# Attention with cosine scores on one core: the written-out instruction orders of the later pairs are replaced

## The chip, the core and the metric

The kernel runs on one core of a Trainium2 chip. The core has five engines with a queue each: TensorE (PE, with its weight loads shown as PEld), VectorE (DVE), ScalarE (ACT), GpSimd (POOL) and SyncE (SP), which issues the transfers. The metric is the device time of one execution in microseconds (us), and the median of several runs is compared.

## The reference

Queries and keys are divided by their norms, the scores are multiplied by 1/tau = 10, and a softmax over the keys weighs the values. There are 8 x 12 heads of 512 positions and 64 dimensions.

```python
Q_norm = Q / (np.linalg.norm(Q, axis=-1, keepdims=True) + 1e-10)
K_norm = K / (np.linalg.norm(K, axis=-1, keepdims=True) + 1e-10)
scores = np.einsum('bhqd,bhkd->bhqk', Q_norm, K_norm) / tau
weights = np.exp(scores - np.max(scores, axis=-1, keepdims=True))
weights = weights / (np.sum(weights, axis=-1, keepdims=True) + 1e-10)
return np.einsum('bhqk,bhkd->bhqd', weights, V).astype(np.float32)
```

## The kernel before

Two heads make a pair, and there are 48 pairs, s = 0 to 47. The work of a pair is a fixed set of operations. The names below are those of the program, and the line is the one that the profile shows.

- LD(s,0), LD(s,1), LV(s): the queries, keys and values are loaded, issued by SyncE (L311, L314). ST(s) stores the result (L569).
- SQ(s,0): GpSimd squares queries and keys at once (L337). RED(s,w): VectorE sums the squares, for w = 0 (queries) and 1 (keys); most sums of the keys are first folded on TensorE by SSQ(s,1) (L354), and then VectorE reduces less (L361 in place of L365).
- NEW(g,k): VectorE finds the reciprocal roots for a group of pairs in steps (L389 to L398).
- SCL(s,w): the scaling to unit length, of queries on VectorE, of keys mostly on GpSimd (both L420).
- TR(s,w): TensorE transposes (L426). EVA(s): VectorE copies the transposes out of the one bank that holds them (L434).
- SCO(s,c): the scores of chunk c (128 keys) for both heads, two matmuls on TensorE (L508).
- EXP(s,c): ScalarE's exponential of those 1024 columns (L531).
- VC(s): GpSimd converts the values (L536).
- PV(s,h,i): four matmuls of the weighted sum (L550); eight such operations make a pair. RCP(s,h) and NRM(s,h): VectorE divides by the sum (L563, L565).

In the pairs 37 and 45 the exponential of chunk 3 isn't ScalarE's. TensorE makes these scores one head at a time in a bank of its own (SCX(s,0), SCX(s,1), L468), VectorE splits each (X(s,h,0), X(s,h,1), L473 and L475), and the polynomial follows: Y(s,0) to Y(s,3) on GpSimd (L479, L480), Y(s,4) and Y(s,5) on VectorE (L486, L480). X(s,0,1) has to be over before SCX(s,1), which writes the same bank.

The scores have two places, so SCO of one chunk waits for the end of the EXP two chunks earlier. PV(s+1,h,0) waits for NRM(s,h), which frees its bank.

Nothing is decided at run time. The dictionary `ORDER` holds one string for each engine, the numbers of the operations in the order in which that engine's queue gets them; a negative number stands for a filler matmul at the start. `Program.schedule` turns the strings into lists, and `write` puts a wait on a semaphore before an operation where another engine has to be done first. Each queue runs strictly in the order written: an operation that waits holds up all behind it on its engine.

```python
for e, text in ORDER.items():
    order[e] = [self.list[int(x)] if x[0] != "-" else self.dummy(int(x[1:])) for x in text.split()]
```

Of the kernel before, what the change touches and what calls it, by code (L numbers as in the profile page):

```python
# [643 lines left out]
def slack(s, most):  # L644
# [14 lines left out]
    ),  # L659
    "pool": (  # L660
# [7 lines left out]
    ),  # L668
    "dve": (
# [24 lines left out]
    ),  # L694
# [33 lines left out]
    ),  # L728
    "act": (
# [44 lines left out]
```

## Time and profile before

| | us |
|---|---|
| median of 3 runs | 189.68 (189.59 to 189.91) |
| the profiled execution | 189.45 |
| its span in the trace | 187.7 |
| ScalarE busy | 180.8 (96%) |
| TensorE busy | 173.8 (93%) |
| VectorE busy | 173.2 (92%) |
| GpSimd busy | 166.8 (89%) |

The span is that of the instructions; what lies around it makes up the rest of the profiled execution's time. Busy times of one engine are a union, so instructions that overlap in their pipeline count once. A row of the timeline gives the start, the time from start to end, the engine, the line, the operation, the tiles and shapes and the count; rows of one line that follow each other are put together.

### The profile page before, as it was taken

The page shows a single profiled execution, that of the slowest core. Times are in us where ns is not written, and L with a number is a line of the kernel's source. Part 1 is how long each engine was busy: PE and PEld are TensorE (multiplying, and loading weights), DVE is VectorE, ACT ScalarE, POOL GpSimd, SP SyncE. Part 2 cuts the span into 40 slices and gives each one's busy share as a digit, 9 for nine tenths or more (in the row PEclk, how much of TensorE's full clock was granted, in tenths as well). Part 3 has the DMA queues.
Part 4 walks back from the last instruction along what each step waited for, and adds up shares of the span by engine and source line. Part 5 has one row for each costly group of instructions (what it writes and reads, how often), then busy time and mean ns, then how long its engine had stood idle before and what let it go on. Part 6 is the DMA issues. An engine that isn't in the chain of part 4 may idle for free.

```text
span 187.7 us, 6646 instructions
## 1 busy us (share of the span) xinstructions
PE 173.8 (93%) x2694; PEld 108.9 (58%) x2694; DVE 173.2 (92%) x546; ACT 180.8 (96%) x212; POOL 166.8 (89%) x152
## 2 busy tenths in 40 slices
PE   6898999999999999999999999999999889998983
PEld 2455666566665666666666556556655446665642
DVE  2788999999999999999999999999999999999864
ACT  4899999999999999999999999999999999999992
POOL 4699999999999999999999999999999999774700
PEclk9999999999999999999999999999999999999999
DMA  5999999899999978999999998899989323112324
GB/s 169 349 351 351 348 357 318 267 326 357 380 386 373 322 248 276 337 334 333 375 380 381 357 334 269 277 291 267 293 279 292 122 88 115 55 61 66 110 65 159
DMA packets 52446, 50.76 MB, mean 270 GB/s; under 512 B 3136, under 2 KB 52416, under 8 KB 52416
## 3 DMA queue, kind: packets, MB, share of 16 engines
q1 hardware_dynamic: 51984, 50.02, 81.2%
q8 instruction: 21, 0.34, 0.8%
q10 hardware_dynamic: 432, 0.33, 0.5%
q14 instruction: 9, 0.07, 0.1%
HBM read 37.75 MB, written 12.58 MB: 268 GB/s over the span
## 4 chain that ended last, share of the span: by engine, by line
ACT 73%; PE 12%; DVE 9%; DMA 3%; issue 1%; SPq 1%
ACT et L531 72%; PE ops L550 4%; PE scps L508 4%; DMA qk<-in_Q_dram 3%; PE tps L426 2%; DVE qn L420 2%; DVE ob L565 2%; DVE xz L475 1%; DVE qt L434 1%; DVE et L486 1%; PE tps L468 1%; DVE xp L473 1%; DVE nps L365 1%; PE ops L580 1%; SPq L311 0%
## 5 line engine op out<-in xcount | busy, mean ns | idle before, releaser
L531 ACT ACTIVATE et<-scps 128x1024 bf16<-128x1024 f32 (+1 forms) x191 | 174.6, 1136 | 0.2
L337 POOL TENSOR_TENSOR sq<-qk 128x1024 bf16<-128x1024 f32 x44 | 82.7, 1892 | 0.6 <-DMA qk<-in_K_dram 0.4
L508 PE MATMUL scps<-qt 64*128 64x512 bf16 x380 | 74.9, 386 | 7.2 <-ACT et L531 3.9
L550 PE MATMUL ops<-vb,et 128*128 128x65 bf16 x1504 | 74.0, 195 | 0.7 <-ACT et L531 0.4
L550 PEld LDWEIGHTS ops<-vb,et 128*128 128x128 bf16 x1504 | 56.0, 98 | 28.6 <-issue 20.9
L420 POOL TENSOR_TENSOR qn<-qk,rk 128x512 bf16<-128x512 f32 x36 | 38.0, 1068 | 2.1 <-DVE rk L394 1.7
L565 DVE TENSOR_TENSOR ob<-ops,rd 128x256 f32<-128x256 f32 x94 | 38.9, 418 | 0.4
L420 DVE TENSOR_TENSOR qn<-qk,nps 128x512 bf16<-128x512 f32 x58 | 38.6, 678 | 0.5 <-ACT nps L382 0.5
L434 DVE COPY qt<-tps 128x1024 bf16<-128x1024 bf16 x47 | 32.2, 686 | 1.9 <-PE tps L426 1.5
L426 PE MATMUL tps<-ident,qn 128*128 128x128 bf16 x376 | 33.7, 221 | 0.2
L508 PEld LDWEIGHTS scps<-qt 64*128 64x128 bf16 x380 | 19.0, 92 | 24.7 <-ACT et L531 10.1
L365 DVE TENSOR_REDUCE nps<-sq 128x8 f32<-128x512 bf16 x48 | 32.3, 683 | 0.0
L536 POOL TENSOR_SCALAR vb<-vf 128x512 bf16<-128x512 f32 x48 | 29.8, 634 | 0.2
L426 PEld LDWEIGHTS tps<-ident,qn 128*128 128x128 bf16 x376 | 21.4, 98 | 12.9 <-issue 6.4
L563 DVE RECIPROCAL rd<-ops 128x4 f32<-128x4 f32 x94 | 16.3, 175 | 3.3 <-PE ops L550 2.5
L354 PE MATMUL ops<-sq,ident 128*128 128x64 bf16 x368 | 18.4, 194 | 0.0
L354 PEld LDWEIGHTS ops<-sq,ident 128*128 128x128 bf16 x368 | 13.8, 98 | 3.4 <-issue 2.3
L361 DVE TENSOR_REDUCE nps<-ops 128x8 f32<-128x64 f32 x40 | 8.5, 213 | 0.1
L480 POOL TENSOR_TENSOR xz<-xz 128x1024 f32<-128x1024 f32 x2 | 3.8, 1892 | 3.4 <-DVE xz L475 3.4
L389 DVE TENSOR_TENSOR nps<-nps,ys 128x32 f32<-128x32 f32 (+1 forms) x30 | 6.3, 209 | 0.1
L390 DVE SCALAR_TENSOR_TENSOR nps<-nps,ys 128x32 f32<-128x32 f32 (+1 forms) x30 | 6.2, 208 | 0.1
L331 POOL TENSOR_TENSOR sq<-qk 128x512 bf16<-128x512 f32 (+1 forms) x4 | 3.7, 932 | 1.0 <-DMA qk<-in_K_dram 0.9
(61 smaller groups left out, 63.7 us busy)
## 6 DMA issues: line engine op xcount, KB each, us to landing
vf<-in_V_dram SPq DMA_DIRECT2D x48, 256.0 KB, 5.3
qk<-in_Q_dram SPq DMA_DIRECT2D x47, 256.0 KB, 4.7
qk<-in_K_dram SPq DMA_DIRECT2D x47, 256.0 KB, 5.6
out_dram<-ob SPq DMA_DIRECT2D x47, 256.0 KB, 4.0
qk<-in_Q_dram SPq DMA_DIRECT2D x2, 128.0 KB, 2.7
qk<-in_K_dram ACTq DMA_DIRECT2D x2, 128.0 KB, 2.9
out_dram<-ob SPq DMA_DIRECT2D x1, 128.0 KB, 1.7
out_dram<-ob ACTq DMA_DIRECT2D x1, 64.0 KB, 1.6
```

What stands on the lines that cost most here:

```text
L337: lambda e: e.tensor_tensor(out=sqf, in0=data, in1=data, op=ALU.mult))
L354: last = e.matmul(out=o_ps[bank][:, 320:384], lhsT=ident[:, :], rhs=sq[iqs][:, 8 * w : 8 * w + 8, 8 * k : 8 * k + 8], start=(k == 0), stop ...
L365: lambda e, w=w, dst=dst: e.tensor_reduce(out=dst, in_=sq[iqs][:, 8 * w : 8 * w + 8, :], axis=AX.X, op=ALU.add))
L420: lambda e, w=w, r=r: e.tensor_tensor(out=qn[iqn][:, w].rearrange("p t h d -> p h t d"), in0=qk[iq][:, w].rearrange("p h (t d) -> p h t d" ...
L426: last = e.transpose(t_ps[:, w, t, :], qn[iqn][:, w, t].rearrange("p h d -> p (h d)"), ident[:, :])
L434: lambda e: e.tensor_copy(out=qt[iqt][:, :, :, :].rearrange("p w t x -> p (w t x)"), in_=t_ps[:, :, :, :].rearrange("p w t x -> p (w t x)")))
L508: last = e.matmul(out=sc_ps[:, 2 * b + h, :], lhsT=qt[iqt][64 * h : 64 * h + 64, 1, c, :], rhs=qt[iqt][64 * h : 64 * h + 64, 0, :, :], sta ...
L531: lambda e, c=c, b=b, hs=hs: e.activation(out=et[iet][:, c, hs[0] : hs[-1] + 1, :], in_=sc_ps[:, 2 * b + hs[0] : 2 * b + hs[-1] + 1, :], f ...
L536: lambda e: e.tensor_scalar(out=vb[:, iq, :, :, 0:DIM].rearrange("p c h d -> p h c d"), in0=vf[iv][:, :, :].rearrange("p h (c d) -> p h c ...
L550: last = e.matmul(out=o_ps[h][:, 65 * t : 65 * t + 65], lhsT=et[iet][:, c, h, 128 * t : 128 * t + 128], rhs=vb[:, iq, c, h, :], start=(i = ...
L563: lambda e, h=h, grid=grid: e.reciprocal(out=rd[io][:, h, :], in_=grid[:, :, DIM]))
L565: lambda e, h=h, grid=grid: e.tensor_tensor(out=ob[io][:, h], in0=grid[:, :, 0:DIM], in1=rd[io][:, h, :].unsqueeze(2).to_broadcast([128, N ...
```

## The change

Only the strings of three engines in `ORDER` differ. ScalarE's and SyncE's stay as they are. The set of operations, their waits, tiles and buffers stay too: the same numbers stand in another order. 389 of TensorE's 735 places, 252 of VectorE's 546 and 71 of GpSimd's 148 hold another operation than before. The first place that differs is TR(15,0), just before the scores of pair 14, on TensorE, RED(19,0) on VectorE and SCL(17,1) on GpSimd.

The core of the diff, GpSimd's string and the last part of TensorE's:

```diff
     "pool": (
...
-        "437 350 395 471 361 318 488 530 426 460 564 607 641 502 536 683 513 717 579 547 759 590 793 836 655 689 "
-        "870 624 666 904 742 731 765 700 938 981 808 819 776 876 1015 1049 910 1083 853 887 921 1125 1066 953 "
-        "1159 987 964 1021 1193 1227 1270 998 1304 1032 1097 1131 1338 1165 1108 1371 1142 1199 1321 1253 1176 "
-        "1414 1459 1242 1210 1493 1397 1526 1310 1343 1287 1603 1421 1386 1637 1569 1465 1354 1670 1712 1436 1757 "
-        "1437 1442 1438 1439 1476 1575 1552 1791 1620 1509 1809 1774 1609 1586 1653 1695 1642 1684 1719 1763 1796 "
+        "437 350 395 471 361 318 488 530 426 460 564 607 641 502 536 683 513 717 579 547 759 590 793 836 655 624 "
+        "870 689 666 904 731 776 700 765 938 887 921 742 808 981 1015 819 998 876 1049 1083 910 853 1125 953 1021 "
+        "987 1032 1159 964 1193 1227 1270 1304 1108 1338 1097 1287 1131 1066 1371 1199 1165 1414 1142 1493 1176 "
+        "1242 1310 1459 1354 1526 1210 1253 1321 1397 1343 1603 1386 1637 1421 1569 1670 1465 1712 1436 1437 1757 "
+        "1438 1442 1439 1476 1575 1791 1509 1695 1552 1609 1740 1586 1653 1620 1642 1809 1684 1719 1774 1763 1796 "
...
     "pe": (
...
-        "1204 1177 1178 1183 1179 1180 1206 1184 1185 1186 1275 1208 1416 1245 1277 1247 1211 1212 1213 1214 1461 "
-        "1249 1311 1217 1309 1251 1218 1219 1220 1279 1344 1342 1281 1254 1260 1255 1256 1283 1261 1262 1257 1263 "
+        "1112 1117 1140 1118 1200 1168 1198 1170 1143 1149 1150 1172 1144 1145 1146 1373 1174 1151 1152 1241 1202 "
+        "1243 1204 1183 1177 1178 1184 1206 1185 1179 1180 1416 1208 1186 1245 1277 1275 1247 1211 1212 1213 1214 "
...
```

Read back into names, TensorE's queue around the scores of pair 35 and of pairs 43 to 47:

```
before: SCO(35,0) PV(33,1,3) SCX(37,0) PV(34,0,0) SCO(35,1) PV(34,0,1) PV(34,0,2) PV(34,0,3) SSQ(41,1)
        SCO(35,2) SCX(37,1) PV(34,1,0) SCO(35,3) PV(34,1,1) PV(34,1,2) PV(34,1,3) SCO(36,0)
after:  SCO(35,0) SCX(37,0) PV(33,1,2) PV(33,1,3) SCO(35,1) PV(34,0,0) PV(34,0,1) SCO(35,2) PV(34,0,2)
        SCX(37,1) SCO(35,3) PV(34,0,3) SSQ(41,1) PV(34,1,0) SCO(36,0)
before: SCO(43,3) PV(42,0,2) SCX(45,1) PV(42,0,3) SCO(44,0) SCO(44,1) ... SCO(45,0) PV(43,1,0) PV(43,1,1)
        TR(47,1) PV(43,1,2) PV(44,0,0) PV(43,1,3) SCO(45,1) TR(47,0) SCO(45,2) PV(44,0,1) PV(44,1,0)
        PV(44,0,2) PV(44,0,3) PV(44,1,1) PV(44,1,2) PV(44,1,3) SCO(46,0) SCO(46,1)
after:  SCO(43,3) PV(42,0,1) PV(42,0,2) SCO(44,0) SCX(45,1) PV(42,0,3) SCO(44,1) ... SCO(45,0) PV(43,1,2)
        PV(43,0,3) PV(43,1,3) SCO(45,1) TR(47,0) TR(47,1) SCO(45,2) PV(44,0,0) PV(44,0,1) PV(44,0,2)
        SCO(46,0) PV(44,0,3) PV(44,1,0) PV(44,1,1) PV(44,1,2) PV(44,1,3) SCO(46,1)
```

GpSimd's queue around the polynomial of pair 37, and VectorE's from X(37,1,1) to the copy of pair 40:

```
GpSimd before: SQ(45,0) Y(37,0) SQ(46,0) Y(37,1) VC(37) Y(37,2) Y(37,3) VC(38) SCL(41,1) VC(40) SQ(47,0)
GpSimd after:  SQ(45,0) Y(37,0) Y(37,1) SQ(46,0) Y(37,2) VC(37) Y(37,3) VC(38) SCL(41,1) SQ(47,0) VC(39)
VectorE before: RCP(34,1) NRM(34,0) X(37,1,1) NRM(34,1) RED(43,0) SCL(39,0) RED(42,1) RCP(35,0) NEW(17,0)
        NRM(35,0) RCP(35,1) NEW(17,1) RED(44,0) NEW(17,2) NRM(35,1) NEW(17,3) SCL(39,1) NEW(17,4) EVA(38)
        NEW(17,5) RED(46,0) RCP(36,1) NEW(17,6) NEW(17,7) NRM(36,1) SCL(41,0) RCP(36,0) NEW(17,8) NRM(36,0)
        EVA(39) SCL(40,1) Y(37,4) SCL(40,0) Y(37,5) EVA(40)
VectorE after:  NRM(34,0) X(37,1,1) RCP(34,1) RED(44,0) RED(43,0) SCL(39,0) RED(42,1) NRM(34,1) RCP(35,0)
        NEW(17,0) NRM(35,0) NEW(17,1) EVA(38) NEW(17,2) SCL(39,1) RCP(35,1) RCP(36,0) NEW(17,3) NRM(35,1)
        NEW(17,4) RED(46,0) EVA(39) NEW(17,5) NRM(36,0) NEW(17,6) NEW(17,7) RCP(36,1) NEW(17,8) SCL(41,0)
        NRM(36,1) SCL(40,1) Y(37,4) SCL(40,0) Y(37,5) EVA(40)
```

Of GpSimd's conversions of values, VC(19), VC(22), VC(23), VC(25), VC(33) and VC(35) stand 7 to 18 places earlier, and VC(27), VC(32) and VC(34) 9 to 16 places later.

82 rows, old and new, of the table ORDER are left out of this document.

## The prediction

> **What bounds the kernel now.** I read the page's groups first. ScalarE's exponentials fill the span, and the idle time put down to them is 0.2 us.
>
> ```profile
> L531 ACT ACTIVATE et<-scps 128x1024 bf16<-128x1024 f32 (+1 forms) x191 | 174.6, 1136 | 0.2
> ...
> L434 DVE COPY qt<-tps 128x1024 bf16<-128x1024 bf16 x47 | 32.2, 686 | 1.9 <-PE tps L426 1.5
> ...
> L563 DVE RECIPROCAL rd<-ops 128x4 f32<-128x4 f32 x94 | 16.3, 175 | 3.3 <-PE ops L550 2.5
> ...
> vf<-in_V_dram SPq DMA_DIRECT2D x48, 256.0 KB, 5.3
> ```
>
> That 0.2 misleads, because the exponentials overlap in their pipeline: one can start late without the engine counting as idle. So I read the chain of work that ended last, in order of time, then the windows restricted to this line, and one exponential alone in the timeline.
>
> ```profile
> 14.79 119.22 ACT et L531 x130
> 134.00 0.04 issue
> ...
> 137.84 0.69 DVE xp L473
> ...
> 154.42 0.42 DVE ob L565
> ...
> 170.22 0.02 issue
> 170.24 11.24 ACT et L531 x12
> ```
>
> ```profile
> 134.00:170.24 36.24, 36.08 (x39) 1.00 0.47 151
> ```
>
> ```profile
> 170.24 1.02 ACT L531 ACTIVATE et<-scps 128x1024 bf16<-128x1024 f32 x1
> ```
>
> Up to 134.00 the rhythm is 119.22 / 130 = 0.917 us for each exponential. From the end at 134.00 to the end of the one that starts at 170.24 (171.26) there are 39 + 1 = 40, which at 0.917 need 36.68; they took 37.26, so 0.58 is lost. The last row's 12 need 1.02 + 11 x 0.917 = 11.11 and took 11.24: 0.13 lost. So about **0.71 us**, 0.37% of the time, is what any order can win on ScalarE, besides a few hundredths hidden in the mean of 0.917. Between the two ScalarE rows the chain runs through TensorE, then through VectorE (from 137.84 to 154.84), then through TensorE again. There the others feed ScalarE too late, though hardly any of them has room:
>
> ```profile
> 135.00:150.00 15.00, 13.89 (x202) 8.17 (x200) 14.78 (x45) 14.99 (x17) 14.88 (x11) 1.00 0.75 239
> ```
>
> The columns are busy times of PE, PEld, DVE, ACT and POOL: VectorE 14.78 of 15, GpSimd 14.88.
>
> The tail cannot change much: the last product's matmuls start 0.05 behind the last exponential's end (183.12 + 1.23 = 184.35), not behind other TensorE work.
>
> ```profile
> 183.12 1.23 ACT L522 ACTIVATE et<-scps 128x256 bf16<-128x256 f32 x3
> ...
> 184.40 0.24 PE L580 MATMUL tps<-vb,et 128*128 128x65 bf16 x2
> ```
>
> **TensorE's part of the change.** A score can start when the exponential two back has ended, and it must start early enough. Prices come from the timeline, start to next start:
>
> ```profile
> 138.34 0.54 PE L550 MATMUL ops<-vb,et 128*128 128x65 bf16 x12
> 138.71 0.40 PE L354 MATMUL ops<-sq,ident 128*128 128x64 bf16 x8
> 139.04 0.39 PE L508 MATMUL scps<-qt 64*128 64x512 bf16 x2
> ```
>
> ```profile
> 169.81 0.39 PE L508 MATMUL scps<-qt 64*128 64x512 bf16 x2
> ```
>
> ```profile
> 174.74 0.40 PE L426 MATMUL tps<-ident,qn 128*128 128x128 bf16 x4
> 175.07 0.39 PE L508 MATMUL scps<-qt 64*128 64x512 bf16 x2
> 175.39 1.03 PE L550 MATMUL ops<-vb,et 128*128 128x65 bf16 x28
> 176.35 0.39 PE L508 MATMUL scps<-qt 64*128 64x512 bf16 x2
> ```
>
> Three PV take 138.71 - 138.34 = 0.37, so 0.123 each. A score takes 175.39 - 175.07 = 0.32. Seven PV ahead of a score take 0.96, which is 7 x 0.123 + 0.10: changing over to a score costs 0.10. A fold (SSQ) or a transpose (TR) ahead of a score takes 0.33, so 0.23 without the change-over. A score of the polynomial's chunk is counted like a score, 0.32.
>
> The limit: the score at 169.81 lets its exponential start at 170.24, 0.43 later, and alone that lasts 1.02. The end is due 2 x 0.917 = 1.83 after the place came free, so a score may start 1.83 - 1.45 = **0.38** after that without loss. Each slot of 0.917 has 0.917 - 0.32 = 0.60 for other work; what is over carries into the next slot.
>
> With the two strings read back into names I added up the slots. From pair 23 on, 23 of 98 slots before hold 0.69 or more, the fullest 0.96 (ahead of SCO(46,0), the row at 175.39) and 0.94 (ahead of SCO(45,1)). After, 11 do, and the fullest has 0.82. Carried from slot to slot, the delay of the score reaches the limit of 0.38 before at SCO(45,1) and SCO(46,0), and 0.37 at four others; over 0.30 it is in 10 slots. After, it never exceeds 0.28 (at SCO(40,2), whose slot is unchanged). The other side is pairs 14 to 22: five slots grow to 0.69 or more from at most 0.59, and the delay rises to 0.28, which still leaves 0.10. The work and its change-overs add up to the same in both. Scores that stand later, behind work that used to wait behind them, cost nothing while the delay stays under 0.38; if 0.1 of other waits falls into the slots at 0.28, each 0.1 more is 0.1 lost.
>
> By TensorE's own time alone the order before loses about 0.1; the rest of the 0.71 comes where a wait on VectorE falls into a slot that is nearly full. In pair 35 SCX(37,0) and SCX(37,1) are involved, in pair 40 NRM(37,1) (the chain's 154.42), at 170.24 SCX(45,1), which stood ahead of SCO(44,0) while X(45,0,1) was running. After, SCX(45,1) stands behind SCO(44,0), and while it waits only PV(42,0,3) and SCO(44,1) queue behind it, whose turn comes later anyway. I count all these as gone but for 0.08 at SCO(40,2) and SCO(41,0), where the queues are unchanged: 0.71 - 0.08 = **0.63**.
>
> **VectorE's part.** Its sum does not change, so an operation moved up makes another late. By the durations queued ahead of it, EVA(s), on which the pair's own scores hang, comes earlier by up to 1.8 us (EVA(39)) or later by up to 1.0 (EVA(23)); EVA(40) to EVA(42) stay put. The waits in the page's rows (1.9 for transposes, 3.3 for products) are where it can win: SCX(37,0) now follows its score at once, which takes 0.2 from TensorE's side and removes the wait of 0.10 ahead of the row at 137.84. Together with a wait of about 0.1 for PV(34,1,3) and one reciprocal (at most 0.175) put behind, I expect X(37,1,1) 0.3 earlier.
>
> **GpSimd and the transfers.** GpSimd hardly pauses, so an operation's time is the sum of what stands ahead of it.
>
> ```profile
> 63.81 2.04 POOL L420 TENSOR_TENSOR qn<-qk,rk 128x512 bf16<-128x512 f32 x2
> ```
>
> ```profile
> 77.27 0.47 SPq L314 DMA_DIRECT2D vf<-in_V_dram  x1
> ```
>
> From SCL(17,1), the second in the first row, I add 1.85 for a square, 1.00 for a scaling, 0.59 for a conversion (durations of the rows below less 0.04 of overlap). VC(25), moved up 15 places, then starts at 82.8; LV(25), issued at 77.27, lands 5.3 later at 82.6: 0.2 of cover. VC(21) and VC(31) end 0.3 and 0.5 before their first product can start. I take zero for all three, since a product late by 0.2 finds its slot's delay under 0.28; if the cover goes, the price is 0 to 0.3. Loads follow stores in SyncE's queue, unchanged.
>
> **The lock.** Two VectorE operations read two SBUF tiles, Y(s,4) and Y(s,5). Pair 37 has them beside GpSimd's work, pair 45 alone:
>
> ```profile
> 142.15 1.89 POOL L480 TENSOR_TENSOR xz<-xz 128x1024 f32<-128x1024 f32 x1
> ...
> 147.46 1.89 POOL L480 TENSOR_TENSOR xw<-xw 128x1024 f32<-128x1024 f32 x1
> 149.44 1.04 POOL L479 TENSOR_SCALAR xw<-xw 128x1024 f32<-128x1024 f32 x1
> 150.56 0.62 POOL L536 TENSOR_SCALAR vb<-vf 128x512 bf16<-128x512 f32 x1
> 151.14 2.00 POOL L420 TENSOR_TENSOR qn<-qk,rk 128x512 bf16<-128x512 f32 x1
> 153.12 1.06 POOL L536 TENSOR_SCALAR vb<-vf 128x512 bf16<-128x512 f32 x1
> 154.15 1.89 POOL L337 TENSOR_TENSOR sq<-qk 128x1024 bf16<-128x1024 f32 x1
> ```
>
> ```profile
> 141.39 0.68 DVE L475 SCALAR_TENSOR_TENSOR xz<-xp,tps 128x512 f32<-128x512 int16 x1
> ...
> 150.70 1.55 DVE L486 SCALAR_TENSOR_TENSOR et<-xz,xw 128x1024 bf16<-128x1024 f32 x1
> ...
> 152.77 0.93 DVE L480 TENSOR_TENSOR et<-et,xp 128x1024 bf16<-128x1024 bf16 x1
> 153.62 0.68 DVE L434 COPY qt<-tps 128x1024 bf16<-128x1024 bf16 x1
> ...
> 177.35 1.23 DVE L486 SCALAR_TENSOR_TENSOR et<-xz,xw 128x1024 bf16<-128x1024 f32 x1
> 178.61 0.69 DVE L480 TENSOR_TENSOR et<-et,xp 128x1024 bf16<-128x1024 bf16 x1
> ```
>
> Beside GpSimd they took 1.55 and 0.93 in place of 1.23 and 0.69, and GpSimd's scaling 2.00 in place of 1.04 (two take 2.04, with 0.04 of overlap) and its conversion 1.06 in place of 0.62. Each waited out the one that came first: Y(37,4) really began 0.32 late, 0.16 before VC(38)'s end. The Trainium skill, "SBUF — State Buffer", section "Who interferes with whom", says that a VectorE instruction with two SBUF inputs and a GpSimd instruction that reads SBUF exclude each other for a whole instruction, and the one issued first wins; these rows agree.
>
> Who comes first after the change? Count from the start of X(37,1,1), 141.39 before. GpSimd starts Y(37,0) 0.76 later, then 1.89 + 0.09 (the dependent step, as from 149.35 to 149.44) + 1.04 + 1.89 + 1.89 + 0.62 + 1.04, less 4 x 0.04: Y(37,3) ends at 9.06, VC(38) lets go at 9.02 + 0.62 - 0.16 = 9.48, SCL(41,1) starts at **9.60**. VectorE reached Y(37,4) at 150.70 - 141.39 = 9.31; with a reciprocal moved behind X(37,1,1) that is 9.4 to 9.48, and up to 0.2 more if EVA(39) waits for TR(39,1), which now stands behind SCO(38,0): 9.4 to 9.65. I take 9.5, ahead of the scaling, so VectorE's loss is about nothing in Y(37,4) and 0.24 in Y(37,5). It is close.
>
> **The rivals.** First, **slower: the lock falls the other way.** If VectorE comes to Y(37,4) after 9.60, SCL(41,1) holds it to 9.60 + 1.04 - 0.16 = 10.48 in place of 9.48, which is 1.0. Then SQ(47,0), now next on GpSimd in place of the short VC(40), is held up by Y(37,4), and as it needs 1.89 in place of 0.62 it holds up Y(37,5): Y(37,4) ends at 11.71, the square about 1.74 later, Y(37,5) begins at 13.31 in place of 11.46. EVA(40) comes 1.85 later than I forecast.
>
> ```profile
> 154.53 0.39 PE L508 MATMUL scps<-qt 64*128 64x512 bf16 x2
> ```
>
> Before, EVA(40) ended at 154.30 and SCO(40,0) started at 154.53. The forecast has EVA(40) earlier by the 0.3 of X(37,1,1) and most of the 0.32 in Y(37,4), less the waits: 0.45. In the rival it ends at 154.30 - 0.45 + 1.85 = 155.70. The score is due by 154.53 + 0.33 - 0.3 at the latest, with ScalarE 0.3 ahead: 154.56. So 1.15 is lost against 0.63 won: +0.5, 190.2; 190.1 to 190.6, as the later stalls go or stay. For it: 0.1 decides. Against it: VectorE came 0.44 ahead of the scaling before. The page's rule makes just this of the new order.
>
> Second, **no change that can be told**: VectorE's stretch from 137.84 to 154.84 stays the bound and only its start moves, by 0.2; with the 0.13 at the end that is 0.33 won: 189.35. For it: 14.78 busy of 15. Against it: several waits for TensorE lie in it.
>
> That the change does not do what it says is excluded: the queues follow the strings.
>
> **How the numbers follow.** The profiled execution, 189.45, lies 0.23 below the median. 189.45 - 0.63 = 188.82, and on the median 189.68 - 0.63 = 189.05; this case's own range is 188.85 to 189.3. About 0.2%, 0.38 us, is what a measurement of this kernel can tell. Chances: forecast 0.57, the lock 0.27, VectorE as the bound 0.16. The range takes in nearly all of the forecast and most of the lock's: 188.85 to 190.4. Faster 0.57, same 0.16, slower 0.27.
>
> **What would show it.** The chain should hold ScalarE's row far beyond 134.00, and 40 exponentials from there should take under 36.9. L486 near 150 should last under 1.4 and L480 on VectorE 0.93. If L486 lasts over 2 us, or the SQ beside it over 3, the lock fell the other way. A new PE row with a long wait for GpSimd's L536 would say that the conversions came too late. PEclk stays at 9 throughout.

## The result and the profile after

The new kernel takes 189.43 us in the median of 22 runs (188.86 to 190.22, and one of 193.24), the kernel before 189.93 in 22 runs beside it. The ratio is 0.997, 95% interval 0.9959 to 0.9981: **faster by 0.3%**, where 0.33% (189.05) was forecast. Now and then a run of either kernel takes some 193 us at a lower granted clock (0.973 in this one), and such runs are left out of the ratios. In a second measurement, with the experiments below, it took 189.60 beside 189.88, ratio 0.9988 (0.9970 to 1.0006), an interval that takes in no change. The sign and the range held; the gain is 0.3 to 0.5 us in place of 0.63.

The profiled execution of the new kernel is the slowest of these but one, 190.22 with a span of 188.3, and it shows the change at its worst. First the groups of its page, and the loads of the values:

```profile
L531 ACT ACTIVATE et<-scps 128x1024 bf16<-128x1024 f32 (+1 forms) x191 | 174.5, 1141 | 0.4
...
L536 POOL TENSOR_SCALAR vb<-vf 128x512 bf16<-128x512 f32 x48 | 29.4, 625 | 1.1 <-DMA vf<-in_V_dram 0.9
...
vf<-in_V_dram SPq DMA_DIRECT2D x48, 256.0 KB, 5.9
```

L536 had 0.2 of idle time before, with no wait named; now GpSimd lost 0.9 to one load. The chain of work that ended last (start, us, what) shows where:

```profile
2.66 5.37 DMA qk<-in_Q_dram
...
15.30 54.06 ACT et L531 x59
...
78.47 5.90 DMA vf<-in_V_dram
84.36 0.07 issue
84.44 0.63 POOL vb L536
...
105.56 21.20 ACT et L531 x23
...
155.41 0.42 DVE ob L565
155.83 0.15 DVE nps L361
155.98 0.65 PE ops L550 x16
156.63 0.32 PE scps L508 x2
156.95 0.59 PE ops L550 x16
157.54 0.23 PE ops L354 x8
157.78 0.34 PE scps L508 x2
...
158.14 25.81 ACT et L531 x28
```

Read like the chain of before: from the end at 69.36 to 106.58, the end of the exponential that starts at 105.56, there are 40 exponentials, 36.68 at 0.917, and they took 37.22: **0.54 lost**, behind VC(25) at 84.44. From 126.76 to 159.16 there are 35, 32.10, in 32.40: **0.30 lost**, all in pair 40. The last 28 need 1.02 + 27 x 0.917 = 25.78 and took 25.81. So before's losses after pair 25 are gone but for pair 40, which lost more, and a new loss stands ahead of them.

The second profile of the same kernel (span 187.6) has no wait of VC(25):

```profile
15.16 137.51 ACT et L531 x150
...
157.40 25.81 ACT et L531 x28
```

150 exponentials run in their rhythm (0.9167), 6 more to 158.42 take 5.75 in place of 5.50, and the rest runs through. **0.25 and 0.03 lost, in place of 0.71 before.** From the start of EXP(3,0) to the end of the span this profile takes 187.6 - 20.51 = 167.1, and before 187.7 - 20.08 = 167.6: 0.5 less.

For the experiments I use one number, the **late sum**: for each exponential from pair 3 on, what lies between its end and the end before it beyond 0.917, added up over the records of the trace (all that is over 0.004). It finds a little more than the chain's arithmetic, since it also counts what hides in the mean:

| kernel | late sum, us | where |
|---|---|---|
| before | 0.80 | pairs 25 to 37: 0.29; 40: 0.12; 43 to 46: 0.39 |
| new, first profile | 0.93 | 21 to 26: 0.56; 40: 0.33; 42: 0.03 |
| new, second profile | 0.28 | 40: 0.25; 42: 0.03 |

The first loads set where all this begins: EXP(3,0) starts at 20.08 before, at 20.60 and 20.51 in the two profiles of the new kernel. The load at the head of the chain took 4.85 and 5.37 in the first two; in the third another load heads the chain. Over the profiles of all runs here it starts between 19.93 and 20.80. The queues are the same up to there, so these differences have nothing to do with the change.

### The profile page after: what moved, and what is told of

It is laid out like the page before. It is cut to its first block, busy times and chain, and to the rows that moved or that the text cites. A ratio compares the mean times of both kernels' runs of the same rounds, so it can differ in the third digit from the quotient of the medians.

```text
span 188.3 us, 6634 instructions
## 1 busy us (share of the span) xinstructions
PE 175.0 (93%) x2694; PEld 109.0 (58%) x2694; DVE 173.1 (92%) x546; ACT 180.8 (96%) x212; POOL 166.7 (89%) x152
## 4 chain that ended last, share of the span: by engine, by line
ACT 57%; DVE 15%; POOL 11%; PE 6%; DMA 6%; issue 2%; SPq 1%
ACT et L531 56%; POOL sq L337 5%; POOL qn L420 4%; DMA vf<-in_V_dram 3%; DMA qk<-in_Q_dram 3%; DVE ob L565 3%; DVE qn L420 3%; DVE nps L365 2%; DVE qt L434 2%; PE ops L550 2%; POOL vb L536 2%; PE scps L508 2%; PE tps L426 2%; DVE rd L563 1%; DVE et L486 1%
## 5 line engine op out<-in xcount | busy, mean ns | idle before, releaser
L550 PE MATMUL ops<-vb,et 128*128 128x65 bf16 x1504 | 74.9, 195 | 1.3 <-DVE ob L565 0.4
L426 PE MATMUL tps<-ident,qn 128*128 128x128 bf16 x376 | 33.0, 220 | 0.6 <-POOL qn L420 0.3
L536 POOL TENSOR_SCALAR vb<-vf 128x512 bf16<-128x512 f32 x48 | 29.4, 625 | 1.1 <-DMA vf<-in_V_dram 0.9
L480 POOL TENSOR_TENSOR xz<-xz 128x1024 f32<-128x1024 f32 x2 | 3.8, 1892 | 3.8 <-DVE xz L475 3.7
```

The source lines that it names most:

```text
L426: last = e.transpose(t_ps[:, w, t, :], qn[iqn][:, w, t].rearrange("p h d -> p (h d)"), ident[:, :])
L536: lambda e: e.tensor_scalar(out=vb[:, iq, :, :, 0:DIM].rearrange("p c h d -> p h c d"), in0=vf[iv][:, :, :].rearrange("p h (c d) -> p h c ...
L550: last = e.matmul(out=o_ps[h][:, 65 * t : 65 * t + 65], lhsT=et[iet][:, c, h, 128 * t : 128 * t + 128], rhs=vb[:, iq, c, h, :], start=(i = ...
```

## The experiments

All orders below are parts of the strings, read back into names. "new" is the changed kernel.

### Which part of the strings pays: the late one alone, the early one alone, TensorE alone

```
first:  before's strings up to VC(24) (GpSimd), RCP(22,0) (VectorE), SSQ(29,1) (TensorE), then new's
second: new's strings up to VC(24), NRM(21,1) and TR(25,1), then before's
third:  before's strings of GpSimd and VectorE, new's of TensorE
```

The first, the late part:

> Up to about pair 23 the queues hold the order before, from there the new one (GpSimd from VC(24), VectorE from RCP(22,0), TensorE from SSQ(29,1)). Theory: the new order wins in the later pairs, where the scores' slots were too full, and loses some 0.2 to 0.56 us in pairs 21 to 26, where GpSimd waits 0.9 us at VC(25) for LV(25). Then this one loses nothing early and wins late: 0.6 to 0.8 us under before, ratio 0.996 to 0.997, and the trace has no late exponential ahead of pair 35. Rival A, the gain comes from the early part: at most 0.2 us under before.

190.02 beside 189.82, ratio 1.0005 (0.9992 to 1.0019): not the gain expected. Its chain:

```profile
2.67 5.56 DMA qk<-in_Q_dram
...
15.50 76.98 ACT et L531 x84
...
111.21 36.78 ACT et L531 x40
...
158.22 25.80 ACT et L531 x28
```

From 92.48 to 112.23 there are 21 exponentials: 19.75 in place of 19.26, so 0.49 lost at the seam, in pairs 24 and 27. From there on 0.29 is late in all (0.27 of it in pair 40), where before loses 0.80. The late part does bring half a microsecond, and the seam takes it back.

The second, the early part:

> The other half: the new order up to about pair 23, the order before from there on. Theory: the wait of GpSimd at VC(25) is there as in the new kernel, and the late slots are full as before: 0.2 to 0.6 us over before, ratio 1.001 to 1.003. Rival A, the gain comes from the early part: 0.3 to 0.5 us under before.

190.84, ratio 1.0053 (1.0038 to 1.0067). The late sum is 1.65: 0.86 at the seam in pairs 24 and 25, then before's list again, stall for stall (0.24 at EXP(44,0), 0.10 at EXP(46,0)). The early part earns nothing of its own. The loss is larger than expected and has another cause: VC(25) did not wait in this profile.

The third, TensorE's string alone:

> Only TensorE's string is new; VectorE and GpSimd keep the order before, so VC(25) is late and never waits. Theory: the slots are even, but VectorE's copies and divisions come in another sequence than TensorE wants them, so part of the gain is lost to waits for VectorE: 0 to 0.4 us under before. Rival C, TensorE's slots are all that matters: 0.6 to 0.8 us under before, as VC(25) does not wait either.

204.99, ratio 1.0808 (1.0784 to 1.0832), far outside both expectations. The page:

```profile
L531 ACT ACTIVATE et<-scps 128x1024 bf16<-128x1024 f32 (+1 forms) x191 | 177.6, 1076 | 13.4 <-PE scps L508 12.4
```

TensorE now asks for transposes, products and sums in an order in which VectorE and GpSimd do not make them. So TensorE's string needs at least one of the others; whether it needs GpSimd's as well as VectorE's wasn't tried. (New's GpSimd and VectorE with before's TensorE would wait for each other in a circle.)

### The load of VC(25)

```diff
- VC(25) SCL(22,1) SQ(27,0) SQ(28,0) SCL(23,1) VC(21)   (new, GpSimd)
+ SCL(22,1) SQ(27,0) SQ(28,0) SCL(23,1) VC(21) VC(25)
```

> The new kernel with one GpSimd entry moved: VC(25) stands behind VC(21), some 6 us later, where its load has landed long before. Theory: GpSimd's wait of 0.9 us for the values goes, and with it the late exponentials EXP(21,0), EXP(22,2) and EXP(26,0), 0.21 + 0.16 + 0.19 = 0.56 us in the profiled execution; 0.3 to 0.56 us under the new kernel, ratio to before about 0.995. Rival B, the wait was peculiar to the one slow execution that was profiled: the same as the new kernel, ratio 0.997.

189.38, ratio 0.9977 (0.9964 to 0.9990); late sum 0.29, all in pairs 40 and 42. The late exponentials of pairs 21 to 26 went as expected, but the ratio is rival B's. Measured again beside later experiments:

> The new kernel with VC(25) behind VC(21), measured a second time as the neighbour of the kernel that fills pair 40. Expected: no wait of VC(25), late exponentials 0.28 to 0.30 us, all in pairs 40 and 42, ratio to the kernel before 0.997 to 0.9985.

189.13 beside 189.79, ratio 0.9972 (0.9960 to 0.9984), late sum 0.27. Its chain is the second profile's of new, 0.25 earlier:

```profile
14.91 137.49 ACT et L531 x150
...
157.10 25.81 ACT et L531 x28
```

And new itself, unchanged:

> The new kernel, unchanged, measured a second time beside the three kernels below. In its first profile GpSimd waited 0.9 us for the load LV(25), which took 5.90 us, and three exponentials were late by 0.56 us together; the rest of its list was pair 40 (0.36). Theory A (the wait hangs on how long that one load takes, which differs from execution to execution): the median stays 0.4 to 0.6 us under the kernel before, 189.3 to 189.5 beside 189.9, and in this profile the wait of VC(25) is somewhere between 0 and 0.9 us, with pair 40 late by 0.3 to 0.4 again. Theory B (the wait is there in every execution): the wait is 0.8 to 1.0 us again and the late exponentials again add up to about 0.9 us.

189.60 beside 189.88, with no wait: the median is 0.28 under before, where 0.4 to 0.6 was expected, and the wait is as theory A has it. Four profiles have new's own order around VC(25): it waited 0.90 and 0 in the two of new, 0 in that of the early part above and 0.53 in that of the lock's experiment, next. GpSimd's and SyncE's timelines in the first:

```profile
82.91 0.62 POOL L536 TENSOR_SCALAR vb<-vf 128x512 bf16<-128x512 f32 x1
84.44 0.63 POOL L536 TENSOR_SCALAR vb<-vf 128x512 bf16<-128x512 f32 x1 [0.90 <-DMA vf<-in_V_dram]
```

```profile
78.04 0.38 SPq L569 DMA_DIRECT2D out_dram<-ob  x1
78.47 0.48 SPq L314 DMA_DIRECT2D vf<-in_V_dram  x1
```

GpSimd was ready at 83.53, the load landed at 84.37. Of new's 33 runs in the two measurements (without the one of 193.24), 6 lie over 189.72; of the 24 with VC(25) moved back, none. So, by the four traces, the wait comes in some executions and not in others; it cost 0.56 where it was 0.90, and 0.18 where it was 0.53. By the medians (0.44 and 0.66 under before, against 0.50 and 0.28) the move can't be told from nothing.

### The lock in pair 37, the other way round

```diff
- Y(37,3) VC(38) SCL(41,1) SQ(47,0)   (new, GpSimd)
+ Y(37,3) SCL(41,1) SQ(47,0) VC(38)
```

> The new kernel with one GpSimd operation moved: VC(38) behind SQ(47,0), so that the queue is Y(37,3), SCL(41,1), SQ(47,0), VC(38). The scaling then comes before VectorE's Y(37,4), as in the rival that the lock falls the other way. Theory A (the lock holds for a whole instruction and whoever comes first has it): Y(37,4) on line 486 lasts about 1.0 to 1.2 us longer than its free 1.23, so 2.0 to 2.4; the square holds up Y(37,5) or is held by it, so that Y(37,5) on line 480 lasts 1.5 to 2.3 in place of 0.93; EVA(40) ends 1.2 to 1.9 us later than 155.29, the exponentials of pair 40 are late by 1 to 1.6 us in place of 0.36, and the median is 0.7 to 1.3 us over the new kernel. Theory B (the engines share the port and each only runs slower): Y(37,4) stays at about 1.55 and Y(37,5) at 0.93, and the median is within 0.2 us of the new kernel's.

191.21, ratio 1.0060 (1.0037 to 1.0083), 1.6 over new beside it, more than the 0.7 to 1.3 expected. The timelines of GpSimd and VectorE:

```profile
150.49 1.04 POOL L420 TENSOR_TENSOR qn<-qk,rk 128x512 bf16<-128x512 f32 x1
151.49 2.87 POOL L337 TENSOR_TENSOR sq<-qk 128x1024 bf16<-128x1024 f32 x1
```

```profile
150.62 2.00 DVE L486 SCALAR_TENSOR_TENSOR et<-xz,xw 128x1024 bf16<-128x1024 f32 x1
...
153.14 1.78 DVE L480 TENSOR_TENSOR et<-et,xp 128x1024 bf16<-128x1024 bf16 x1
```

The scaling came 0.13 ahead of Y(37,4), ran its free 1.04, and Y(37,4) took 2.00. The square then waited for Y(37,4) (2.87 in place of 1.89) and Y(37,5) for the square (1.78). Each loser ends where the winner's end, less 0.16, plus its own free time would put it: 151.53 - 0.16 + 1.23 = 152.60 against 152.62. This is the rule of the Trainium skill, "SBUF — State Buffer", section "Who interferes with whom", that the one issued first keeps the other out for a whole instruction; the runs agree, in both directions. EVA(40) ended 1.28 later against X(37,1,1) than in new, as expected, but pairs 39 and 40 were late by 2.8. What is beyond the lock is mostly TensorE's clock. In the windows (columns as in the prediction, then the granted clock, the DMA share and GB/s) and on TensorE's timeline:

```profile
157.00:159.00 2.00, 2.00 (x31) 1.47 (x28) 1.37 (x4) 1.20 (x2) 2.00 (x4) 0.50 0.42 134
```

```profile
157.18 0.61 PE L508 MATMUL scps<-qt 64*128 64x512 bf16 x2
```

The granted clock was 0.50 here, and SCO(40,1) took 0.61 in place of 0.39; SCO(40,2) started 2.49 later against X(37,1,1) than in new. Ahead of it, from 150 to 155, TensorE had been busy for 3.30 of 5.00 us, in the second profile of new for 4.67; what brings the clock down isn't shown. Of the six runs the three with a mean clock of 0.990 or 0.991 took 191.40 to 191.61, those with 0.998 to 1.000 took 190.10 to 191.03. So by the runs at full clock the lock itself costs 0.5 to 1.4 over new; the rest comes with the slower clock.

### Pair 40: three ways to win its 0.25

All three start from new with VC(25) moved. In the first, both transposes of pair 41 fill TensorE's wait for NRM(37,1):

```diff
- SCO(40,0) PV(38,1,0..3) SCO(40,1) PV(38,0,0..3) SSQ(45,1) SCO(40,2) TR(41,1) TR(41,0) SCO(40,3)
+ SCO(40,0) TR(41,1) TR(41,0) PV(38,1,0) SCO(40,1) PV(38,1,1..3) PV(38,0,0) SCO(40,2)
+ PV(38,0,1..3) SSQ(45,1) SCO(40,3)
```

> The new kernel with two edits: the conversion VC(25) behind VC(21) on GpSimd, and in pair 40 the transposes TR(41,1) and TR(41,0) ahead of PV(38,1,0), whose wait of 0.25 us for VectorE's NRM(37,1) they then fill, with the PV and SSQ(45,1) that stood in front of SCO(40,1) and SCO(40,2) spread over the slots behind. Theory A (pair 40's loss of 0.26 us in SCO(40,1) and SCO(40,2) is TensorE's wait for NRM(37,1) plus two full slots): both come in time, the late exponentials add up to less than 0.1 us in place of 0.29, and the median falls 0.2 to 0.3 us below that of the kernel with VC(25) alone, to 0.7 us under the kernel before, ratio 0.996 to 0.997. Theory B (VectorE is the bound there and NRM(37,1) late by itself): the lateness moves to PV(38,1,*) or EVA(41) behind it and the sum stays at 0.25 to 0.35 us; ratio 0.9977 as with VC(25) alone.

189.56, ratio 0.9985 (0.9975 to 0.9994). EXP(40,1) and EXP(40,2) came in time, and EXP(41,0) was late by 0.65; the late sum is 0.72. Three of the four PV(38,1,i) had gone behind a score, and VectorE made RCP(38,1) and what follows later: theory B. Its chain begins with the shortest first load of all:

```profile
2.67 4.67 DMA qk<-in_Q_dram
```

The second moves less:

```diff
+ SCO(40,0) TR(41,1) PV(38,1,0..3) SCO(40,1) PV(38,0,0..3) SCO(40,2) SSQ(45,1) TR(41,0) SCO(40,3)
```

> The new kernel with VC(25) behind VC(21) as before, and in pair 40 only two TensorE operations moved: TR(41,1) ahead of PV(38,1,0), into the 0.2 us for which that product waits for NRM(37,1), and SSQ(45,1) behind SCO(40,2). The four PV(38,1,*) keep their time, unlike in the kernel whose edits of pair 40 made them 0.3 us later on VectorE's clock and EVA(41) 0.43 us later. Theory A (a slot that holds a wait of 0.2 us and 0.82 us of work is over full, and filling the wait with a transpose frees the next slot): SCO(40,2) starts 0.2 to 0.3 us earlier, its exponential is late by less than 0.05 us in place of 0.23, EVA(41) is no later, all late exponentials add up to 0.05 to 0.12 us, and the median is 0.15 to 0.25 us under that of VC(25) alone, ratio to the kernel before 0.9960 to 0.9975. Theory B (VectorE's queue up to EVA(41) is the bound in pair 40, and TensorE only shows it): the 0.25 us come back at EXP(41,0), the sum stays at 0.25 us or more and the median at that of VC(25) alone.

189.65, ratio 0.9991 (0.9978 to 1.0005). Again EXP(40,2) was in time and EXP(41,0) late, by 0.43; late sum 0.49. TensorE's and VectorE's timelines:

```profile
156.53 0.28 PE L550 MATMUL ops<-vb,et 128*128 128x65 bf16 x4
156.74 0.39 PE L508 MATMUL scps<-qt 64*128 64x512 bf16 x2
157.06 0.41 PE L354 MATMUL ops<-sq,ident 128*128 128x64 bf16 x8
...
158.44 0.34 PE L550 MATMUL ops<-vb,et 128*128 128x65 bf16 x6 [0.42 <-DVE nps L361]
```

```profile
157.51 0.18 DVE L563 RECIPROCAL rd<-ops 128x4 f32<-128x4 f32 x1
157.73 0.42 DVE L565 TENSOR_TENSOR ob<-ops,rd 128x256 f32<-128x256 f32 x1
158.07 0.22 DVE L361 TENSOR_REDUCE nps<-ops 128x8 f32<-128x64 f32 x1
```

The products of PV(38,0,3) end at 156.81, but RCP(38,0) starts at 157.51, 0.04 behind the end of SSQ(45,1) at 157.47. SSQ(45,1) writes into the tile of PV(38,0,i), and line 562 makes the reciprocal wait for it too. I had moved the fold as if nobody waited for it: the 0.2 won on TensorE came back as 0.42 ahead of PV(39,0,0), which stands in front of SCO(41,0).

The third takes the lock away. VC(38) also waits for Y(37,4), so that GpSimd is idle beside it:

```diff
- [("LV", s), key("PV", s - R_QK, 0, NT - 1), key("PV", s - R_QK, 1, NT - 1), "vone"]
+ [("LV", s), key("PV", s - R_QK, 0, NT - 1), key("PV", s - R_QK, 1, NT - 1), "vone"] + ([("Y", 37, 4)] if s == 38 else [])
- TR(40,0) PV(37,1,2) SCO(39,3) PV(37,1,3) PV(37,0,3)   (TensorE)
+ TR(40,0) PV(37,1,2) PV(37,1,3) SCO(39,3) PV(37,0,3)
```

> The new kernel with VC(25) behind VC(21), and the lock of pair 37 taken away by a wait: VC(38) on GpSimd also waits for VectorE's Y(37,4), so that GpSimd is idle while Y(37,4) runs, and SCL(41,1) comes behind both; and PV(37,1,3), which needs Y(37,5), stands ahead of SCO(39,3). Theory A (Y(37,4) and Y(37,5) are longer only because of the GpSimd operation that came first, and through PV(37,1,3), RCP(37,1) and NRM(37,1) this is what makes pair 40 late): Y(37,4) on line 486 takes 1.23 in place of 1.5, Y(37,5) on line 480 about 0.7 in place of 0.93, EVA(40) ends 0.2 to 0.5 us earlier against X(37,1,1), NRM(37,1) 0.2 to 0.4 earlier, the wait of 0.2 ahead of PV(38,1,0) goes, and pair 40's late exponentials fall from 0.25 to 0.1 or less; GpSimd is 1.3 to 1.5 us later, which its wait of 0.95 at SCL(44,1) takes up for the most part; sum of late exponentials 0.1 to 0.15, median 0.1 to 0.2 us under that of VC(25) alone, ratio 0.9965 to 0.997. Theory B (GpSimd has no time to give: VC(38) for PV(38,1,0), or SCL(41,1) and SCL(42,1) for the transposes, come too late): the wait ahead of PV(38,1,0) stays or moves to TR(42,1) or EVA(43), the sum is 0.3 or more, ratio 0.9977 or more.

189.26 beside 189.83, ratio 0.9970 (0.9957 to 0.9984), late sum 0.25; by the ratio it can't be told from VC(25) alone. GpSimd's, VectorE's and TensorE's timelines:

```profile
152.14 0.63 POOL L536 TENSOR_SCALAR vb<-vf 128x512 bf16<-128x512 f32 x1 [1.63 <-DVE et L486]
```

```profile
150.76 1.22 DVE L486 SCALAR_TENSOR_TENSOR et<-xz,xw 128x1024 bf16<-128x1024 f32 x1
...
152.50 0.80 DVE L480 TENSOR_TENSOR et<-et,xp 128x1024 bf16<-128x1024 bf16 x1
...
156.08 0.70 DVE L365 TENSOR_REDUCE nps<-sq 128x8 f32<-128x512 bf16 x1 [0.15 <-POOL sq L337]
```

```profile
157.93 0.64 PE L550 MATMUL ops<-vb,et 128*128 128x65 bf16 x16 [0.18 <-POOL vb L536]
```

The lock is gone from Y(37,4) (1.22) and costs Y(37,5) 0.1 (0.80 in place of 0.69), EVA(40) and NRM(37,1) come 0.37 and 0.38 earlier against X(37,1,1), and pair 40 is in time. But EXP(41,0) is late by 0.19: PV(39,0,0), ahead of SCO(41,0), waits again. The view names GpSimd, but VC(39) had long been done; PV(39,0,0) starts 0.15 behind the end of RED(45,1), just as in the other two (158.07 + 0.22 = 158.29 and 158.44 above). RED(45,1) itself is only 0.04 earlier against X(37,1,1) than in new with VC(25) moved, where NRM(37,1) is 0.38 earlier: on the way RED(47,1) waits 0.15 for GpSimd's SQ(47,0), which the idling made late. In all three the loss moved to pair 41, through VectorE's queue up to RED(45,1), and each edit had put a wait into that queue: ahead of RCP(38,1), of RCP(38,0) and of RED(47,1). With VC(25) moved alone VectorE has no idle time over 0.15 there, so that it takes up no such wait. Whether an edit without one would win the 0.25 wasn't tried.

### The stalls of pairs 43 to 46 by TensorE's local edits

Before's kernel with two operations moved, and with all of new's TensorE order from SCO(43,3) on:

```diff
- SCO(43,3) PV(42,0,2) SCX(45,1) PV(42,0,3) SCO(44,0) SCO(44,1)
+ SCO(43,3) PV(42,0,2) SCO(44,0) SCX(45,1) PV(42,0,3) SCO(44,1)
```

> The kernel before with one TensorE edit of two operations: SCX(45,1) and PV(42,0,3) behind SCO(44,0) in place of ahead of it. Theory A (the score SCO(44,0) was late only because SCX(45,1) stood ahead of it and waited 0.32 us for VectorE's X(45,0,1)): EXP(44,0) comes in time, 0.24 us of late exponentials go, SCX(45,1) starts 0.2 to 0.35 us later, VectorE's X(45,1,*) with it, and the rest of the list stays; sum 0.55 in place of 0.80, median 0.2 to 0.3 us under the kernel before, ratio 0.9985. Theory B (any TensorE order needs VectorE's string made for it): X(45,1,0) and the reciprocals of pair 42 behind it come 0.3 us later, and that comes back as late exponentials in pairs 44 to 46; sum 0.8 or more, ratio 1.0 or more.

189.97 beside 189.79, ratio 1.0016 (1.0001 to 1.0030). EXP(44,0) came in time, as expected: 0.24 gone. VectorE's timeline:

```profile
169.99 0.69 DVE L473 TENSOR_SCALAR xp<-tps 128x512 int16<-128x512 f32 x1 [0.35 <-PE tps L468]
```

X(45,1,0) now waits 0.35 for SCX(45,1), 0.20 more than before, so VectorE is 0.18 later from there on, while ScalarE is 0.24 ahead: EXP(44,3) is late by 0.20 and EXP(45,1) by 0.23. Late sum 0.94.

> The kernel before with TensorE's string alone changed from SCO(43,3) on: SCX(45,1) and PV(42,0,3) behind SCO(44,0), the PV of pairs 43 and 44 spread behind later scores, as in the new kernel. VectorE's and GpSimd's strings are those of before. Theory A (a score is late where its TensorE slot is over full, or where a wait on VectorE stands ahead of it): the late exponentials of SCO(44,0) 0.24, SCO(45,1) 0.03 and SCO(46,0) 0.11 go, 0.37 us in all, the rest of before's list (0.43 us) stays, and the median falls by 0.3 to 0.4 us, ratio 0.998. Theory B (only the three strings together bring anything, as TensorE's whole string alone made it 15 us slower): VectorE's products and reciprocals of pairs 42 to 46 are now asked for in another order than they are made, and the sum of the late exponentials does not fall; ratio 1.0 or more.

190.47, ratio 1.0030 (1.0015 to 1.0046), late sum 1.48: EXP(44,0) and EXP(46,0) in time, but 0.20 at EXP(45,0) and 0.79 at EXP(45,2). TensorE's timeline:

```profile
175.84 0.62 PE L426 MATMUL tps<-ident,qn 128*128 128x128 bf16 x8 [0.89 <-DVE qn L420]
```

TR(47,0) waits for SCL(47,0), which in before's VectorE string stands behind RCP(43,0), and that waits 0.83 for PV(43,0,3), which the new order had put back. Both edits take away the stalls that stood first and lose more elsewhere: theory B in both. In new, where VectorE's string was changed with them, the same edits leave nothing of the 0.39 late in these pairs.

## Why the prediction was right, and where it was not

**What bounds the kernel: right.** Lateness on ScalarE is what the change won: the medians moved by 0.5 and 0.3, and in the second profile 0.28 of the 0.71 is left. That no order can win more isn't shown.

**TensorE's slots: right in their place, wrong as a cause by themselves.** All stalls of pairs 25 to 37 and 43 to 46 went, the one behind SCX(45,1) among them, and no score of pairs 14 to 22 was late for a full slot. But the same edits without VectorE's string won nothing in three experiments. The sum of slots told where the gain would lie, not what earned it. Which moves on VectorE and GpSimd earned it wasn't taken apart. One reading was wrong: the slot of SCO(41,0) isn't unchanged, it holds four PV in place of three; EXP(41,0) came in time all the same.

**The term that was mis-sized: what is left in pair 40.** I counted 0.08 and it is 0.25, 0.17 more; the late sum fell by 0.80 - 0.28 = 0.52, not by 0.63. The step that failed is the lock's clock. Against EXP(3,0), X(37,1,1) came 0.31 earlier in the second profile, as forecast (0.3), and Y(37,4) arrived 9.41 and 9.48 after it (forecast 9.4 to 9.65). But the timelines of the first profile say that GpSimd was later than my 9.48 and 9.60:

```profile
149.72 0.63 POOL L536 TENSOR_SCALAR vb<-vf 128x512 bf16<-128x512 f32 x1
150.42 1.04 POOL L479 TENSOR_SCALAR xw<-xw 128x1024 f32<-128x1024 f32 x1
151.55 0.62 POOL L536 TENSOR_SCALAR vb<-vf 128x512 bf16<-128x512 f32 x1
152.13 2.00 POOL L420 TENSOR_TENSOR qn<-qk,rk 128x512 bf16<-128x512 f32 x1
```

```profile
142.26 0.68 DVE L475 SCALAR_TENSOR_TENSOR xz<-xp,tps 128x512 f32<-128x512 int16 x1
...
151.66 1.57 DVE L486 SCALAR_TENSOR_TENSOR et<-xz,xw 128x1024 bf16<-128x1024 f32 x1
153.16 0.68 DVE L420 TENSOR_TENSOR qn<-qk,nps 128x512 bf16<-128x512 f32 x1
153.76 0.93 DVE L480 TENSOR_TENSOR et<-et,xp 128x1024 bf16<-128x1024 bf16 x1
```

Y(37,3) and VC(38) each start about 0.08 behind the end of what stands ahead of them (149.72 + 0.63 = 150.35; 150.42 + 1.04 = 151.46), where I had taken 0.04 off. The prediction's own rows of before show it for VC(38): 149.44 + 1.04 = 150.48, and the next starts at 150.56. So the scaling came at 9.88 and the conversion let go near 9.75: Y(37,4) lost 0.34 in place of nothing, 1.57 as before's 1.55, and not under the 1.4 that I had named as the sign. EVA(40) came 0.18 earlier than before (second profile, against EXP(3,0)), not 0.45, and TensorE waited 0.2 for NRM(37,1) ahead of PV(38,1,0). The experiment that took the lock away from Y(37,4), and moved PV(37,1,3) one score ahead so that RCP(37,1) can follow, shows that this is the lock's doing: the wait and pair 40's lateness went.

**The rival of the lock** was held to be closer than it was: VectorE came 0.47 ahead of the scaling. Its mechanism stands: the experiment made it happen. Its price, 1.15 over the forecast, lies within the 0.5 to 1.4 over new of the runs at full clock, though there VC(38) stood behind the square, too; that TensorE's clock would fall with it, which made it 1.6 in the median, was in no term.

**The transfers: the step with a real miss.** "Loads follow stores in SyncE's queue, unchanged" is true and not enough. ST(16) stands ahead of LV(25), and it waits for NRM(16,1), which the change moved back on VectorE; against EXP(3,0) the load was issued 0.67 later than before, while VC(25) was ready only 0.2 later than I had it. So the 0.2 of cover had become a lack of 0.3 for a transfer of the 5.3 counted, and the transfer's own time decides: 5.90 made the wait 0.90, and in the second profile, with no wait, it was at most 5.0 (issued 78.36, VC(25) at 83.38). I gave a price of 0 to 0.3; it was 0.56 in the first profile.

**The signs.** L480 on VectorE took the 0.93 named, PEclk stayed at 9, and the 40 exponentials behind 134.00 take 36.68 + 0.25 = 36.93 in the second profile, just over the 36.9.

**The other rival**, VectorE as the bound, has something in it: in pairs 40 and 41 VectorE has no time to spare, and the 0.25 there did not yield to three tries. The medians can't decide: of the 0.50 and 0.28 won, one lies halfway between its 0.33 and the forecast's 0.63 and the other beside the 0.33. The traces do: with the rival, VectorE's stretch from 137.84 on stays in the chain; in the second profile ScalarE's row holds to 152.67, and between there and the tail VectorE is in the chain only at pair 40.

A version that is faster than before in both its measurements is new with VC(25) behind VC(21): 0.9977 and 0.9972, against 0.997 and 0.9988 of new. What it may have over new is the missing tail of long executions (none of 24 over 189.72, against 6 of 33); by the medians the two can't be told apart.

## What to carry to other kernels

Where an engine is busy 96%, count its lateness from the spacing of its ends, not from its idle time: 0.80 us were late in before, and the page put 0.2 down. Strings of several queues written by hand are one object: each edit of TensorE's order alone took its own stall away and lost as much or more elsewhere, as long as the other strings were made for another order. Before moving an operation, list who waits for it: the reciprocal for a fold in the same tile, a load behind a store behind a division.

## What the hardware showed that was not expected

The same first load of the chain took between 4.67 and 5.56 us in different executions, and that moves the whole span by as much as the change wins; LV(25) took 5.90 and at most 5.0 in the two profiles of new. A cover of 0.2 us for such a transfer is none. TensorE's granted clock went to 0.50 for some 3 us in one profile, behind a stretch with pauses of up to 0.86, and a score took 0.61 in place of 0.39: a stall on another engine can cost more than its own length. On GpSimd, VC(38) and, in its place, SCL(41,1) start 0.08 behind the end of Y(37,3), on which neither depends, where other neighbours overlap by 0.04; why was not found.
